# A trunk layer on one Trainium2 core: its loads bound to program order on the sync queue

## The chip, the cores and the metric

One NeuronCore of a Trainium2 chip runs the whole program. The metric is the device time of one execution in microseconds (us). The kernel before takes 1918.01 us in the median of 3 runs (1916.22 to 1918.19). The engines are named as in the profile: PE (TensorE), PEld (its weight loads), DVE (VectorE), ACT (ScalarE), POOL (GpSimd), and SP (SyncE), which here only issues DMAs.

## What is computed

One layer for 512 tokens of width 2048: sliding-window attention with grouped keys and a learned sink, then a gated feed-forward part with a causal convolution of width 3, each between two RMS norms and with a residual. The part that the change touches is the second:

```python
def conv_ffn(h, w_up, conv_w, w_down):
    S = h.shape[1]
    u = h @ w_up                                   # 512x2048 @ 2048x11264
    up = jnp.pad(u, ((0, 0), (CONV_WIDTH - 1, 0), (0, 0)))
    c = conv_w[0] * up[:, 0:S]
    for j in range(1, CONV_WIDTH):
        c = c + conv_w[j] * up[:, j:j + S]
    gate, val = jnp.split(c, 2, axis=-1)
    return (jax.nn.silu(gate) * val) @ w_down      # 512x5632 @ 5632x2048
```

All is float32. The kernel splits every matrix into a high part `wh` (what PE's fast 32-bit format holds) and a rest `wl`, and forms each product with three matmuls: high by high, high by low, low by high (`prod`, L88 to L92; the matmuls all carry L83).

## The kernel before

Attention and its output projection come first (until about 510 us). Then come two stages. **Up stage**: the 5632 gate and value columns are made in 44 groups of 128, f = 0 to 43. Groups 4 to 43 are made by `up_pair(f, g)`, with a scheme of Strassen's kind: seven products of half size in place of eight. A pair (the gate and the value columns of f) loads four blocks of 128x1024 weights (`block`, tile `bw`, six buffers, 512 KB each), makes seven forms of them with DVE adds into a tile `raw`, splits each form into `wh` (ACT, L64) and `wl` (DVE, L65) in a ring of five slots, and multiplies each by a prepared form of the activations: 7 x 8 x 3 = 168 matmuls with 256 columns. Results are copied from PSUM by ACT (`s1`, `s2`, `s3`, `s7` at L672, `uv` at L704). At its end `gate` (L572 to L579) convolves both halves (`c0`, `c1`: one ACT step at L567, two DVE steps at L568 and L569 each), applies the SiLU on ACT (L574), multiplies on DVE (L576) and stores the result from SP into the DRAM tensor `hd` (L578).

**Down stage**: seven products of the same scheme again. Their weight operands are rows of the down matrix (`in_wdn`) and sums of them. These sums were made during the earlier stages, for each of the 22 row pairs kp, and stored in the DRAM tensor `td`: four loads of 512 KB into tiles `ts` (a pool of four), four adds, four stores. `weight_sums` adds on DVE (L144); `queue_sums` lets the DMA add into its target (L151, L152). In the up stage every five groups start one set of each kind: `weight_sums` at i = f - 4 = 0, 5, ..., 35 ahead of the pair, `queue_sums` after pair i = 1, 6, ..., 36; kp 6 to 21 are made so. All of these loads, adds and stores are issued by POOL. After the last set the `ts` pool is closed, its room becomes the tile `hq10`, and `fetch` brings the first activations of the down stage there. In the down stage `weight_form` loads `raw` (four buffers) and `fetch` loads the rest of the activations (`hq`), one piece every second kp.

What sets the order: matmuls are bound to the order in which they are traced (`keep_in_program_order`, in `mm`). Every other instruction is placed by a scheduler, which may move it ahead of others on its engine as far as its data and buffers allow. Each engine then works through its own list in that fixed order and waits at an instruction whose inputs are not there. SP does so too: a DMA issue that waits holds up those behind it.

Of the kernel before, what the change touches and what calls it, by code (L numbers as in the profile page):

```python
# [14 lines left out]
ALU = mybir.AluOpType  # L15
# [26 lines left out]
def trunk(ctx, tc, xT, x, grow, table, onehot, masked, sinks, conv,  # L42
          wkv, wq, wo, wup, wdn, out):
    nc = tc.nc
# [12 lines left out]
    def bank(i):  # L57
        return ps.tile([P, 512], F32, name=f"b{i}", bufs=1)
# [4 lines left out]
    def split(hi, lo, src):  # L63
        nc.scalar.activation(hi, src, AF.Copy)  # L64
        nc.vector.tensor_tensor(lo, src, hi.bitcast(F32), ALU.subtract)  # L65

    def halves():
        p = ring["slots"][ring["next"] % len(ring["slots"])]
        ring["next"] += 1
        return p.tile([P, 1024], F32R, name="wh"), p.tile([P, 1024], F32R, name="wl")  # L70
# [64 lines left out]
    hd = dr.tile([2, 2, P, NP, HALF], F32, name="hd")  # L135
    td = dr.tile([NP, P, 4, 1024], F32, name="td")

    def weight_sums(kp, sums):
        t = [sums.tile([P, 1024], F32, name="ts") for _ in range(4)]
        for q in (0, 2, 1, 3):  # L140
            nc.gpsimd.dma_start(t[q], wdn[4 * kp + q])
        yield
        for q, o in ((2, 0), (0, 1), (1, 2), (3, 1)):
            nc.vector.tensor_tensor(t[q], t[q], t[o], ALU.add)  # L144
            nc.gpsimd.dma_start(td[kp, :, q, :], t[q])
            yield

    def queue_sums(kp, sums):
        t = [sums.tile([P, 1024], F32, name="ts") for _ in range(4)]
        for q, other in ((2, 0), (0, 1), (1, 2), (3, 1)):  # L150
            nc.gpsimd.dma_start(t[q], wdn[4 * kp + q])  # L151
            nc.gpsimd.dma_start(t[q], wdn[4 * kp + other] if q in (0, 2) else t[other], accum_op=ALU.add)  # L152
            nc.gpsimd.dma_start(td[kp, :, q, :], t[q])

    def step(g, n=1):
        for _ in range(n):
            next(g, None)

    with ExitStack() as att:
# [10 lines left out]
        with ExitStack() as ph:  # L170
# [26 lines left out]
            for kt in range(KT):  # L197
                if kt == 0:
                    for h in range(2):
                        r = first[:, KT:] if h == 0 else pa.tile([P, 512], F32, name="xs")  # L200
                        c = KT + h * S
                        nc.sync.dma_start(r if h else first, xT[:, c if h else 0:c + S])
                        if h == 0:
                            w = halves()
                            raw = wraw.tile([P, 1024], F32, name="raw")
# [4 lines left out]
                elif kt % 2 == 0:  # L210
                    r = pa.tile([P, 1024], F32, name="xr")
# [205 lines left out]
        for u in range(NKV * NT):  # L417
            t = Unit(u)
# [28 lines left out]
    with ExitStack() as op:  # L447
        sums = op.enter_context(pool("tso", 4))
# [5 lines left out]
        g1 = gp.tile([P, D], F32, name="g1")  # L454
# [42 lines left out]
        def oproj(d, o):  # L497
            for u in range(8):
                w = weights(wo, 8 * d + u)
                for b in range(NT):  # L500
                    for k in range(2):
                        kt = 2 * u + k
                        prod(o[b], station(b, kt), wide(w, k), kt == 0, kt == KT - 1)
                if u % 4 == 0:
                    g = weight_sums(2 * d - 2 + u // 4, sums)
                step(g, (1, 0, 2, 3)[u % 4])
            for b in range(NT):
                evac_m(b, d, o[b])
# [9 lines left out]
        for b, bk in enumerate((2, 5, 6, 7)):  # L518
            o = bank(bk)
            for kt in range(KT):  # L520
                prod(o, station(b, kt), wide(ws[kt // 2], kt % 2), kt == 0, kt == KT - 1)
                if b > 1:
                    turn_tok(b - 2, kt, (0, 1, 3, 4))
                if b < 2:
                    if kt == 0:
                        g = weight_sums(4 + b, sums)
                    if kt in (0, 9, 11, 13, 15):
                        step(g)
            evac_m(b, 3, o)
            xn[b] = finish_tok(b)  # L530

        wu = {(h, u): weights(wup, 2 * h + u) for h in range(4) for u in range(2)}
        o = [bank(k) for k in (0, 1, 2, 5)]
# [18 lines left out]

    def fetch(m, par, g0, g1):
        t, k0 = next((t, k) for t, k, k1 in hq[m, par] if k <= g0 < k1)
        nc.sync.dma_start(t[:, g0 - k0:g1 - k0, :], hd[m, par, :, g0:g1, :])

    with ExitStack() as us:
        fp = us.enter_context(pool("fp", 1))
# [93 lines left out]
        sums = tsu.enter_context(pool("tsu", 4, side="right"))  # L652

        def block(f, r, c):
            t = bw.tile([P, 1024], F32, name="bw")
            nc.sync.dma_start(t, wup[4 * f + 2 * c + r])
            return t

        def form(t):
# [15 lines left out]
        def up_pair(f, g):  # L675
            X, Y, Z = (bank(k) for k in ((0, 1, 6), (3, 4, 7))[f % 2])
            ug = un.tile([P, S], F32, name="ug", bufs=2)
            uv = un.tile([P, S], F32, name="uv", bufs=2)
            b11, b21 = block(f, 0, 0), block(f, 1, 0)
            t = wraw.tile([P, 1024], F32, name="raw")  # L680
            nc.vector.tensor_tensor(t, b11, b21, ALU.add)
            times(X, 2, form(t), True)
            s1 = shot(X, "s1")
            step(g)
            b12 = block(f, 0, 1)
            times(Z, 7, form(b12), True)
            s7 = shot(Z, "s7")
            nc.vector.tensor_tensor(t, t, b12, ALU.add)
            times(X, 5, form(t), False)
            s2 = shot(X, "s2")  # L690
            step(g)
            nc.vector.tensor_tensor(b11, b11, b12, ALU.add)
            times(Z, 6, form(b11), False)
            b22 = block(f, 1, 1)
            nc.vector.tensor_tensor(t, t, b22, ALU.add)
            times(X, 3, form(t), False)
            s3 = shot(X, "s3")
            step(g)
            nc.vector.tensor_tensor(ug[:, :HALF], Z[:, :HALF], s2, ALU.subtract)
            times(Y, 1, form(b21), True)  # L700
            nc.vector.tensor_tensor(uv[:, :HALF], s3, s7, ALU.subtract)
            times(X, 4, form(b22), False)
            nc.vector.tensor_tensor(ug[:, HALF:], s1, Y[:, :HALF], ALU.subtract)
            nc.scalar.activation(uv[:, HALF:], X[:, :HALF], AF.Copy, scale=-1.0)  # L704
            gate(f, (ug, uv))

        kp = 6
        for f in range(4, NF):
            i = f - 4
            if i % 5 == 0 and kp < NP:  # L710
                work = weight_sums(kp, sums)
                step(work)
                kp += 1
            up_pair(f, work if i % 5 == 1 else iter(()))
            if i % 5 == 1:
                step(work)
            if i % 5 == 1 and kp < NP:
                queue_sums(kp, sums)
                kp += 1
            if kp == NP and tsu:  # L720
                tsu.close()
                tsu = None
                early = ctx.enter_context(pool("early", 1, side="right"))
                hq[1, 0] = [(early.tile([P, 16, HALF], F32, name="hq10"), 0, 16)]
                for g0, g1 in batches[:4]:
                    fetch(1, 0, g0, g1)
# [38 lines left out]
    def weight_form(src, kp):  # L765
        raw = raws[kp % 2].tile([P, 1024], F32, name="raw")
        table, q = src
        nc.sync.dma_start(raw, td[kp, :, q, :] if table else wdn[4 * kp + q])
        hi, lo = halves()
        split(hi, lo, raw)  # L770
        return hi, lo
# [5 lines left out]
    def product(o, form, src, fresh, tail=0):  # L777
        kept = []
        for g0, g1 in batches:
            af = act_form(*form, g0, g1)  # L780
            for kp in range(g0, g1):
                wf = weight_form(src, kp)
                if coming and kp % 2 == 0:
                    fetch(*coming.pop(0))
                if kp >= NP - tail:
                    kept.append((kp, af, g0, wf))
                    continue
                for t in range(2):
                    for e in range(2):
                        multiply(o, kp, af, g0, wf, t, e, fresh)  # L790
        return kept
# [13 lines left out]
    sums = {}  # L805
# [121 lines left out]
```

## Time and profile before

| | us |
|---|---|
| median of 3 runs | 1918.01 |
| the profiled execution, whole | 1915.05 |
| the profiled execution, first to last instruction (span) | 1913.3 |
| PE busy in the span | 1862.9 |
| DVE busy | 1455.1 |
| ACT busy | 980.9 |
| POOL busy | 125.9 |

All durations are taken from the profiled execution; its own time is 1.8 us more than its span and 3 us less than the median. The up pairs run from about 625 to 1458 us, the down stage from there to the end. PE's granted clock is a share of 2.4 GHz: 1.00, or 0.50 at the lower level. Where an engine is idle, the profile names what released it.

### The profile page before, as it was taken

How to read it: one execution, taken by the hardware profiler on the slowest of the kernel's cores; microseconds unless marked ns; L12 is line 12 of the kernel's file. 1: busy time of each engine (PE TensorE's matmuls, PEld its weight loads, DVE VectorE, ACT ScalarE, POOL GpSimd, SP SyncE). 2: the span in 40 equal slices, each digit the busy share in tenths (PEclk: the TensorE clock that was granted, in tenths of full speed). 3: DMA queues.
4: the chain of work that ended last, by engine and by line, in shares of the span. 5: the costliest groups of instructions: out<-in, count | busy, mean ns of one | idle time of the engine just before them, and what ended most of it. 6: DMA issues, size and time to landing. Idle time of an engine off the chain costs nothing.

```text
span 1913.3 us, 30053 instructions
## 1 busy us (share of the span) xinstructions
PE 1862.9 (97%) x11822; PEld 1689.4 (88%) x11822; DVE 1455.1 (76%) x2047; ACT 980.9 (51%) x1566; POOL 125.9 (7%) x216
## 2 busy tenths in 40 slices
PE   9999999999999999999999999999996899999998
PEld 7888888888899999998999999999996788888886
DVE  5468888745788979987898988888885466666875
ACT  7357777622344535444454555555553455545553
POOL 0000000012100222222222000000000000000000
PEclk9999999999999999999999999999998999999999
DMA  9533234499643889999999443333335766676773
GB/s 312 149 97 102 93 113 158 144 344 337 242 165 127 273 280 321 304 312 301 329 306 303 166 127 111 126 124 112 127 99 214 261 196 202 189 234 192 236 249 119
DMA packets 120845, 392.02 MB, mean 205 GB/s; under 512 B 13216, under 2 KB 26752, under 8 KB 118784
## 3 DMA queue, kind: packets, MB, share of 16 engines
q1 hardware_dynamic: 86720, 271.84, 42.2%
q0 software_dynamic: 29952, 109.07, 17.8%
q10 hardware_dynamic: 4032, 9.21, 1.6%
q8 instruction: 92, 1.51, 0.3%
q14 instruction: 49, 0.40, 0.1%
HBM read 309.29 MB, written 72.39 MB: 199 GB/s over the span
## 4 chain that ended last, share of the span: by engine, by line
PE 68%; DMA 16%; issue 9%; DVE 6%; ACT 1%; POOL 1%; DVEq 0%; SPq 0%; ACTq 0%; POOLq 0%
PE b L83 66%; DMA ts<-in_wdn 4%; DMA bw<-in_wup 3%; DMA ts<-ts 2%; DVE wl L65 2%; DMA raw<-in_wo 2%; PE b L86 1%; DMA td<-ts 1%; ACT wh L64 1%; DVE ts L144 1%; DMA hq<-hd 1%; DMA raw<-td 0%; DMA raw<-in_wup 0%; DVE xt L482 0%; DVE c L569 0%
## 5 line engine op out<-in xcount | busy, mean ns | idle before, releaser
L64 ACT ACTIVATE wh<-raw 128x1024 fp32r<-128x1024 f32 (+1 forms) x371 | 388.2, 1055 | 489.9 <-PE b L83 267.4
L65 DVE TENSOR_TENSOR wl<-raw,wh 128x1024 fp32r<-128x1024 f32 (+1 forms) x371 | 449.3, 1219 | 231.7 <-ACT wh L64 231.0
L83 PE MATMUL b<-ah,wh 128*128 128x256 f32 (+1 forms) x1824 | 561.9, 308 | 0.9 <-ACT s L672 0.5
L83 PE MATMUL b<-ah,wl 128*128 128x256 f32 (+1 forms) x1824 | 555.8, 305 | 5.9 <-DVE wl L65 5.9
L83 PE MATMUL b<-al,wh 128*128 128x256 f32 (+1 forms) x1824 | 554.4, 304 | 0.4 <-DVE al L65 0.4
L83 PEld LDWEIGHTS b<-ah,wl 128*128 128x128 f32 x1824 | 348.8, 191 | 22.3 <-DVE wl L65 7.7
L83 PEld LDWEIGHTS b<-ah,wh 128*128 128x128 f32 x1824 | 349.3, 192 | 13.2 <-ACT wh L64 2.0
L83 PEld LDWEIGHTS b<-al,wh 128*128 128x128 f32 x1824 | 349.4, 192 | 11.0 <-DVE al L65 0.6
L83 PE MATMUL b<-wh 128*128 128x512 f32 x616 | 241.7, 392 | 19.9 <-ACT wh L64 19.4
L83 PE MATMUL b<-wl,wh 128*128 128x512 f32 x616 | 241.9, 393 | 1.2 <-DVE wl L65 1.2
L83 PE MATMUL b<-wh,wl 128*128 128x512 f32 x616 | 241.4, 392 | 0.0
L64 ACT ACTIVATE wh<-bw 128x1024 fp32r<-128x1024 f32 x160 | 167.6, 1055 | 120.4 <-PE b L83 120.3
L65 DVE TENSOR_TENSOR wl<-bw,wh 128x1024 fp32r<-128x1024 f32 x160 | 194.3, 1219 | 7.6 <-ACT wh L64 7.0
L83 PEld LDWEIGHTS b<-wh 128*128 128x128 f32 x616 | 116.8, 190 | 45.6 <-ACT wh L64 20.3
L83 PEld LDWEIGHTS b<-wl,wh 128*128 128x128 f32 x616 | 116.7, 189 | 26.3 <-DVE wl L65 2.0
L83 PEld LDWEIGHTS b<-wh,wl 128*128 128x128 f32 x616 | 116.8, 190 | 24.2
L83 PE MATMUL b<-wh,ah 128*128 128x512 f32 x320 | 126.5, 395 | 0.0
L83 PE MATMUL b<-wh,al 128*128 128x512 f32 x320 | 124.8, 390 | 0.0
L83 PE MATMUL b<-wl,ah 128*128 128x512 f32 x320 | 124.6, 389 | 0.0
L144 DVE TENSOR_TENSOR ts<-ts 128x1024 f32<-128x1024 f32 x56 | 68.4, 1221 | 40.2 <-DMA ts<-in_wdn 31.8
L672 ACT ACTIVATE s<-b 128x256 f32<-128x256 f32 x160 | 59.3, 371 | 73.9 <-PE b L83 73.9
L83 PE MATMUL b<-f6h,wh 128*128 128x256 f32 x320 | 92.3, 288 | 5.0 <-ACT s L672 5.0
(165 smaller groups left out, 3099.4 us busy)
## 6 DMA issues: line engine op xcount, KB each, us to landing
bw<-in_wup SPq DMA_DIRECT2D x160, 512.0 KB, 4.8
ts<-in_wdn POOLq DMA_DIRECT2D x104, 512.0 KB, 8.3
td<-ts POOLq DMA_DIRECT2D x88, 512.0 KB, 5.5
raw<-td SPq DMA_DIRECT2D x88, 512.0 KB, 4.7
raw<-in_wdn SPq DMA_DIRECT2D x66, 512.0 KB, 4.2
raw<-in_wq SPq DMA_DIRECT2D x32, 512.0 KB, 3.6
raw<-in_wo SPq DMA_DIRECT2D x32, 512.0 KB, 4.8
hd<-c SPq DMA_DIRECT2D x44, 256.0 KB, 4.5
```

What stands on the lines that cost most here:

```text
L64: nc.scalar.activation(hi, src, AF.Copy)
L65: nc.vector.tensor_tensor(lo, src, hi.bitcast(F32), ALU.subtract)
L83: tc.keep_in_program_order(nc.tensor.matmul(o, l, r, start=start, stop=stop, skip_group_check=more))
L86: tc.keep_in_program_order(nc.tensor.transpose(o, src, ident))
L144: nc.vector.tensor_tensor(t[q], t[q], t[o], ALU.add)
L672: nc.scalar.activation(t, o[:, :HALF], AF.Copy)
```

## The change

A helper `in_turn` issues a DMA on SP and binds it behind the instruction that was traced just before it on SP. It is used for the `bw` loads, the down stage's `raw` loads, the activation loads of `fetch`, and the `ts` loads of the up stage, which leave POOL's queue for SP's. `queue_sums` issues its four loads first and its adds and stores after them in another order. The stores `hd` are not bound, nor are the weight sums of the stage before (kp 0 to 5). Line numbers behind the helper rise by 3 to 16.

```diff
+    def in_turn(o, i):
+        tc.keep_in_program_order(nc.sync.dma_start(o, i))
+
-    def weight_sums(kp, sums):
+    def weight_sums(kp, sums, paced=False):
         t = [sums.tile([P, 1024], F32, name="ts") for _ in range(4)]
         for q in (0, 2, 1, 3):
-            nc.gpsimd.dma_start(t[q], wdn[4 * kp + q])
+            (in_turn if paced else nc.gpsimd.dma_start)(t[q], wdn[4 * kp + q])
...
     def queue_sums(kp, sums):
         t = [sums.tile([P, 1024], F32, name="ts") for _ in range(4)]
-        for q, other in ((2, 0), (0, 1), (1, 2), (3, 1)):
-            nc.gpsimd.dma_start(t[q], wdn[4 * kp + q])
-            nc.gpsimd.dma_start(t[q], wdn[4 * kp + other] if q in (0, 2) else t[other], accum_op=ALU.add)
+        for q in (2, 0, 1, 3):
+            in_turn(t[q], wdn[4 * kp + q])
+
+        def add(q, o):
+            nc.gpsimd.dma_start(t[q], o, accum_op=ALU.add)
+
+        def store(q):
             nc.gpsimd.dma_start(td[kp, :, q, :], t[q])
+
+        add(2, wdn[4 * kp])
+        add(0, wdn[4 * kp + 1])
+        store(2)
+        add(1, t[2])
+        store(0)
+        add(3, t[1])
+        store(1)
+        store(3)
...
     def fetch(m, par, g0, g1):
-        nc.sync.dma_start(t[:, g0 - k0:g1 - k0, :], hd[m, par, :, g0:g1, :])
+        in_turn(t[:, g0 - k0:g1 - k0, :], hd[m, par, :, g0:g1, :])
...
         def block(f, r, c):
-            nc.sync.dma_start(t, wup[4 * f + 2 * c + r])
+            in_turn(t, wup[4 * f + 2 * c + r])
...
-                work = weight_sums(kp, sums)
+                work = weight_sums(kp, sums, True)
...
     def weight_form(src, kp):
-        nc.sync.dma_start(raw, td[kp, :, q, :] if table else wdn[4 * kp + q])
+        in_turn(raw, td[kp, :, q, :] if table else wdn[4 * kp + q])
```

What stands where, at three places. First SP's list around pairs 7 and 8. Pair 7 loads bw_6655, 6657, 6691 and 6783 and its gated product is c1_6881; pair 8 loads bw_6892, 6894, 6928 and 7020 (c1_7118); pair 9 loads bw_7137, 7139, 7173 and 7265; pair 10 begins with bw_7374 and 7376. Before:

```order
L656 DMA bw_6894<-in_wup 128x1024
L578 DMA hd_88<-c1_6389 128x2x256
L656 DMA bw_6928<-in_wup 128x1024
L656 DMA bw_7020<-in_wup 128x1024
L656 DMA bw_7137<-in_wup 128x1024
L656 DMA bw_7139<-in_wup 128x1024
L578 DMA hd_88<-c1_6644 128x2x256
L656 DMA bw_7173<-in_wup 128x1024
L656 DMA bw_7265<-in_wup 128x1024
L656 DMA bw_7374<-in_wup 128x1024
L656 DMA bw_7376<-in_wup 128x1024
L578 DMA hd_88<-c1_6881 128x2x256
```

After, at the same pairs:

```order
L139 DMA bw_6655<-in_wup 128x1024
L139 DMA bw_6657<-in_wup 128x1024
L139 DMA bw_6691<-in_wup 128x1024
L139 DMA bw_6783<-in_wup 128x1024
L594 DMA hd_88<-c1_6881 128x2x256
L139 DMA bw_6892<-in_wup 128x1024
L139 DMA bw_6894<-in_wup 128x1024
L139 DMA bw_6928<-in_wup 128x1024
L139 DMA bw_7020<-in_wup 128x1024
L594 DMA hd_88<-c1_7118 128x2x256
```

The store of a pair's product stood behind the first loads of three pairs later, and now stands between the pair's own loads and the next pair's.

Second, DVE's list at the end of pair 7 (ug_6653, uv_6654 are its results, c0_6876 and c1_6881 its gate) and the beginning of pair 8 (its forms are built in raw_6896). Before:

```order
L65 TENSOR_TENSOR wl_6899<-raw_6896,wh_6898 128x1024
L144 TENSOR_TENSOR ts_7127<-ts_7127,ts_7125 128x1024
L699 TENSOR_TENSOR ug_6653<-b7_6652,s2_6752 128x256
L65 TENSOR_TENSOR wl_6931<-bw_6928,wh_6930 128x1024
L701 TENSOR_TENSOR uv_6654<-s3_6814,s7_6721 128x256
L688 TENSOR_TENSOR raw_6896<-raw_6896,bw_6928 128x1024
L703 TENSOR_TENSOR ug_6653<-s1_6689,b4_6651 128x256
L681 TENSOR_TENSOR raw_7141<-bw_7137,bw_7139 128x1024
L65 TENSOR_TENSOR wl_6962<-raw_6896,wh_6961 128x1024
L65 TENSOR_TENSOR wl_6993<-bw_6892,wh_6992 128x1024
L568 SCALAR_TENSOR_TENSOR c1_6881<-uv_6654,cw_83,c1_6881 128x511
```

After:

```order
L584 SCALAR_TENSOR_TENSOR c0_6876<-ug_6653,cw_83,c0_6876 128x511
L585 SCALAR_TENSOR_TENSOR c0_6876<-ug_6653,cw_83,c0_6876 128x510
L584 SCALAR_TENSOR_TENSOR c1_6881<-uv_6654,cw_83,c1_6881 128x511
L585 SCALAR_TENSOR_TENSOR c1_6881<-uv_6654,cw_83,c1_6881 128x510
L592 TENSOR_TENSOR c1_6881<-c0_6876,c1_6881 128x512
L697 TENSOR_TENSOR raw_6896<-bw_6892,bw_6894 128x1024
L708 TENSOR_TENSOR bw_6892<-bw_6892,bw_6928 128x1024
L65 TENSOR_TENSOR wl_6899<-raw_6896,wh_6898 128x1024
```

Splits and sums of pair 8 stood among the last steps of pair 7; now the first of them stands behind pair 7's product, and ACT's list follows in the same way.

Third, SP's list where the last weight sums give way to `hq10`, at the entry into pair 41 (bw_14946). After:

```order
L139 DMA ts_14918<-in_wdn 128x1024
L139 DMA ts_14916<-in_wdn 128x1024
L139 DMA ts_14917<-in_wdn 128x1024
L139 DMA ts_14919<-in_wdn 128x1024
L139 DMA hq10_14936<-hd_88 128x1024 x4
L139 DMA bw_14946<-in_wup 128x1024
L139 DMA bw_14948<-in_wup 128x1024
```

Before, three of these hq10 loads stood among the loads of pairs 25 and 26 and the fourth some 40 rows later, since POOL had the sums done by then; the ts loads were not in SP's list.

## Rows read from the trace of the kernel before

**Rows 1.** Windows: length, busy us (instructions) of PE, PEld, DVE, ACT, POOL; clock; DMA.

```profile
690.00:1080.00 390.00, 371.75 (x3024) 368.61 (x3023) 341.11 (x377) 189.71 (x274) 82.99 (x136) 0.98 0.93 300
1080.00:1456.00 376.00, 375.65 (x3131) 375.45 (x3129) 318.32 (x351) 198.81 (x280) 0.00 (x0) 1.00 0.36 115
```

**Rows 2.** Waits of PE from 604 to 1456: us in total, times, longest.

```profile
PE b L83 <- ACT s L672: 9.9, 8, 3.3
PE b L83 <- DVE wl L65: 8.3, 6, 2.4
```

**Rows 3.** Waits of PE from 1456 to 1503, the change of stage.

```profile
PE b L83 <- ACT wh L64: 19.4, 2, 15.4
```

**Rows 4.** Timeline of SP in the quiet part: start us, us, instruction.

```profile
1162.64 0.38 SPq L578 DMA_DIRECT2D hd<-c  x1
...
1182.80 0.38 SPq L578 DMA_DIRECT2D hd<-c  x1
```

**Rows 5.** Waits of SP from 604 to 1456, at the stores.

```profile
SPq L578 <- DVE c L576: 48.0, 36, 3.7
```

**Rows 6.** Timeline of PE after pair 43.

```profile
1458.16 0.28 PE L83 MATMUL b<-f4h,wl 128*128 128x256 f32 x1
...
1477.35 0.79 PE L83 MATMUL b<-wh 128*128 128x512 f32 x1 [15.41 <-ACT wh L64]
```

**Rows 7.** Timelines of ACT, DVE and SP at the gate of pair 43.

```profile
1458.51 0.36 ACT L704 ACTIVATE uv<-b 128x256 f32<-128x256 f32 x1
1458.90 0.72 ACT L567 ACTIVATE c<-uv,cw 128x512 f32<-128x512 f32 x1
1460.79 0.63 ACT L574 ACTIVATE c<-c 128x512 f32<-128x512 f32 x1 [1.17 <-DVE c L569]
...
1460.67 0.74 DVE L568 SCALAR_TENSOR_TENSOR c<-uv,cw,c 128x511 f32<-128x511 f32 x1
1461.45 0.75 DVE L569 SCALAR_TENSOR_TENSOR c<-uv,cw,c 128x510 f32<-128x510 f32 x1
1462.31 0.69 DVE L576 TENSOR_TENSOR c<-c,c 128x512 f32<-128x512 f32 x1
...
1463.17 0.38 SPq L578 DMA_DIRECT2D hd<-c  x1
1463.59 2.60 SPq L555 DMA_DIRECT2D hq<-hd  x4
```

**Rows 8.** Tile bw from 604.4 to 608.3, a burst of loads: issues, and landing.

```profile
L656 SPq DMA_DIRECT2D bw<-in_wup x6: 327/456/919, 604.5 to 607.8; - x6
...
DMA to landing us min/median/max: 3.9/7.0/8.4
```

**Rows 9.** Tile bw from 1150 to 1260: ns min/median/max, first and last start.

```profile
L65 DVE TENSOR_TENSOR wl<-bw,wh x22: 1216/1220/1226, 1149.4 to 1256.2; 128x1024 fp32r<-128x1024 f32 x22
...
L692 DVE TENSOR_TENSOR bw<-bw x6: 1220/1224/1225, 1154.2 to 1255.1; 128x1024 f32<-128x1024 f32 x6
...
DMA to landing us min/median/max: 3.4/3.6/4.1
```

**Rows 10.** DMA issues from 640 to 1080: count, size, median us to landing.

```profile
bw<-in_wup SPq DMA_DIRECT2D x82, 512.0 KB, 7.0
...
td<-ts POOLq DMA_DIRECT2D x63, 512.0 KB, 6.3
ts<-ts POOLq DMA_DIRECT2D x16, 512.0 KB, 8.5
```

**Rows 11.** Windows at the lower clock and after it, columns as in rows 1.

```profile
697.00:703.80 6.80, 6.23 (x29) 6.23 (x30) 6.80 (x8) 3.17 (x6) 1.62 (x4) 0.50 0.59 198
703.80:711.00 7.20, 7.20 (x62) 7.20 (x62) 5.49 (x7) 0.53 (x2) 1.95 (x3) 1.00 0.97 284
...
908.60:915.40 6.80, 5.58 (x26) 5.58 (x27) 6.80 (x8) 0.48 (x2) 1.61 (x3) 0.50 0.79 280
...
1477.30:1482.00 4.70, 4.18 (x9) 3.00 (x10) 4.67 (x4) 2.95 (x3) 0.00 (x0) 0.50 1.02 413
```

## The prediction, on record before the change was run

> **What bounds the kernel now.** I read the windows by stage first. In the up stage TensorE (PE) is nearly always busy: 371.75 of 390 us while weight sums are also being made, 375.65 of 376 us after them [rows 1]. So only its waits can be won back there. The list of PE's waits gives them: 9.9 us for ScalarE (ACT) copies out of PSUM and 8.3 us for VectorE (DVE) splits [rows 2]. The third view is the change from the up to the down stage, where PE waits 19.4 us for weight halves, 15.4 of them at once [rows 3]. All of the rest is matmuls. One up pair (168 matmuls) lasts 20.16 us when nothing waits: that is the distance of two stores of gated activations [rows 4]. Between those stores PE never stops, because the loads of a pair run ahead of the pair before: bw has six buffers and a pair takes four.
>
> **What the change does to the queue.** Each bound load is put behind whatever was traced just before it on SP. At a pair's first load that is the store hd of the pair before, whose product is the last thing the pair makes. The order on SP shows it: before, the loads of pairs 8 and 9 and two of pair 10 stand ahead of the store of pair 7; now the store of pair 7 stands ahead of every load of pair 8. SP goes through its list in order and does wait at this store (36 waits in the up stage, for the DVE product) [rows 5]; those waits hurt nobody while loads stood ahead. The order on DVE and ACT follows: the sum of pair 8's first two blocks now stands behind pair 7's product. So at all 40 entries into an up pair (f = 4 to 43) nothing of the next pair is ready when PE ends its last matmul, and PE drains. I read this from the order, and price it from the trace.
>
> **The price of a plain entry.** The trace of before holds one such drain, at the end of pair 43: last matmul 1458.16 + 0.28 = 1458.44; 3.5 us later (1477.35 - 15.41 = 1461.94) the one block that was ready is used up, and PE stands until 1477.35 [rows 6]. Its steps, counted from the last matmul's end [rows 7]: the ACT copy uv starts at 0.07; the convolution's ACT step starts 0.39 later, and the SiLU (0.63) now stands between them; it lasts 0.72: 1.81. Two DVE convolution steps and the product go from 1460.67 to 1463.00, 2.33: 4.14. SP issues the store 0.17 later: 4.31, and its next DMA 0.42 after that: 4.73.
>
> Then loads. There is one burst of six bw loads on a quiet DMA, with one hd store among them [rows 8]: the first lands 3.9 us after its issue, the last at 607.8 + 8.4 = 616.2, that is 7.8 us after the first for five loads and half a load, 1.42 us each. The first form needs blocks one and two, but DVE's second instruction adds block three into block one and the split of the first form stands behind that. So the third load counts: 4.73 + 3.9 + 2 x 1.42 = 11.47. An add (1.22) and a split (1.22) follow [rows 9]: 13.9 us of idle PE.
>
> Then the clock. PE restarts at 1477.35 at a granted clock of 0.50 (1.2 GHz) and has 2.4 GHz again at 1482.0 [rows 6, 11]. At the lower level a 256-column matmul comes every 6.23/29 = 0.215 us, at the upper 7.2/62 = 0.117 [rows 11]; 4.7 us there lose 4.7 x (1 - 0.117/0.215) = 2.1. A plain entry costs 13.9 + 2.1 = 16.0 us. Three in five are plain: 24 x 16.0 = 384.
>
> The Trainium skill, TensorE: Matmul & The Clock Gate, section HAM oscillation, describes a kernel whose every tile restarts at the lower clock after a wait for data. By that rule all 40 entries pay the 2.1; if only this one place did, the sum would be 84 lower. The trace bears the rule out at this place and at 697 and 908.6.
>
> **Entries with weight sums in front.** Eight groups of five pairs make two sets of sums. Their four ts loads were on POOL's queue; they now stand on SP between the store and the next pair's loads, once per set: 16 entries. Four loads more before the third bw load: 4 x 1.42 = 5.7. POOL's queue moves the sums' stores and adds at the same time. While both queues were full, a bw load took 7.0 us [rows 10] against 3.6 in quiet [rows 9], so the share of that lies between 0 and 3.4; I take the middle, 1.7, since POOL has no loads left. 16.0 + 5.7 + 1.7 = 23.4, for 15 of them 351.
>
> The Trainium skill, DMA: Bandwidth & Descriptors, section Queues, rings and completion order, says that an engine goes round the queues that have work, a packet from each. By that the loads would get half the engines for as long as POOL has work, the upper end: 3.4 in place of 1.7, 26 us more over the 15. Rows 10 agree in kind.
>
> The sixteenth is the entry into pair 41: the loads hq10 stand there, in a tile over the room of the ts pool, so SP holds until the last sums are stored. First ts load 4.73 + 3.9 = 8.6; three adds that follow one another, 8.5 each [rows 10]: 34.1; a store, 6.3: 40.4; then four hq10 loads and three bw loads, 3.9 + 6 x 1.42 = 12.4: 52.8; add and split 2.4, clock 2.1: 57. Before, POOL was done by 1080 [rows 1], and nobody waited for this.
>
> **What is won.** The contention that delayed bw goes, with PE's 18.2 us [rows 2] and two spells of 6.8 us at the lower clock, 3.0 each [rows 11]: 24. At the change of stage the down weights no longer stand behind twelve hq loads: of 19.4 + 2.1 us I expect some 13 to stay, because block kp 0 is split only after the last gate and kp 1 is loaded after the last store: 8 won. In the down stage the loads keep their order but for neighbours that change places, and PE is the bound there: nothing. Instructions on PE, their number and order are the same.
>
> **Sum.** 384 + 351 + 57 = 792 lost, 24 + 8 = 32 won: 760 more. The profiled execution took 1915.05 us, 3 under the median of 1918.01: 1915 + 760 + 3 = **2678 us**.
>
> Lower bound of an entry: landing in 3.4 [rows 9], two loads enough for a start, 4.73 + 3.4 + 1.42 + 1.22 + 1.22 = 12.0, and no clock loss: 24 x 12.0 + 15 x 17.7 + 40 = 594, about 2480 in all. Upper bound: the store takes its half load's 0.7 first, a whole 6.8 us spell at the lower clock costs 3.0, sums 3.4: 17.6 and 26.7, the last 75: 898, about 2785.
>
> **The rivals.**
> - *The loads are paced and nobody drains.* If the first loads of a pair could go out before the store of the pair before is due, the change would only keep sums from crowding bw, and win its 24 + 8 us: about 1886. For it: SP's waits for the product summed to only 48 us [rows 5]. Against it: the order, in all 40 places, and DVE's order with it. It is decided by whether SP's first load of a pair is issued before or after the last matmul of the pair before. 4 in 100. No change at all: 1.
> - *The clock never recovers within a pair.* PE would work some 20 us and rest 14, and the lower level could hold through all 168 matmuls: 168 x (0.215 - 0.117) = 16.5, less the 2.1 counted, 14.4 x 40 = 576: about 3250. Against it: recovery 4.7 us after 15.4 of idling [rows 6, 11]. 6 in 100.
> - *The drain is real but shorter*, since first matmuls or the gate's steps overlap with something that I don't see: between 2000 and 2480: 7 in 100, mostly near the upper end.
>
> **How the numbers follow.** My forecast with its bounds has 82 in 100. The range is 2520 to 2810: the bounds with most of both ends, a little above the upper one, for the 16 entries with sums, whose price is a middle. About 0.2% is what a measurement of this kernel tells from no change. Faster by more: 0.04; within: 0.01; slower: 0.95.
>
> **What would show it.** Per pair, SP should issue hd and then four bw loads within 2 us, some 4.3 us after the last matmul; hd stores should lie 36 us apart, 43 with sums; PE's list of waits should be led by about 40 x 14 us or more in the up stage (wh and wl of the first form); the granted clock should fall in each drain; one pause of 55 us should stand before pair 41; POOL should issue 64 fewer loads; the down stage should last the same 410 us. Wrong would be: bw loads issued during the pair before, or PE without gaps in the up stage.

## The result, and the profile after

The changed kernel takes **2664.53 us** (median of 4 runs, 2660.88 to 2667.32), 1.389 times the kernel before (95% interval 1.387 to 1.392): 39% slower. 2678 was predicted. The profiled execution took 2660.88 us, its span is 2659.1 us. All line numbers from here on are those of the changed kernel, unless a kernel is said to be made from the one before.

From the page: PE's busy time, share and instructions; PE and its granted clock in 40 slices of the span; the chain that ended last, by engine.

```profile
PE 1964.8 (74%) x11822; PEld 1772.9 (67%) x11822; DVE 1486.4 (56%) x2047; ACT 982.1 (37%) x1566; POOL 91.5 (3%) x152
...
PE   9999999997466466566565665665665368999998
...
PEclk9999999998688678778777777777777688999999
...
PE 71%; DMA 13%; DVE 8%; ACT 3%; SPq 3%; issue 2%; POOL 0%; DVEq 0%; ACTq 0%; POOLq 0%
```

PE has the same 11822 matmuls, and is busy 1964.8 us against 1862.9. Idle it is 2659.1 - 1964.8 = 694.3 us, against 50.4. Both rows of slices have a hole where the up pairs lie, and nowhere else. Two windows of the up stage, with the columns of [rows 1]:

```profile
690.00:1080.00 390.00, 225.60 (x1658) 219.95 (x1657) 185.83 (x197) 102.47 (x148) 15.81 (x24) 0.77 0.34 115
1080.00:1456.00 376.00, 222.17 (x1634) 216.90 (x1632) 178.40 (x190) 101.83 (x145) 15.89 (x24) 0.78 0.34 113
```

PE issues 1658 matmuls where it issued 3024, and DMA is used about a third (0.34): nothing is saturated, everything waits in turn. PE's waits from 604 to 2220 us (in total, times, longest) say on what, and SP's on its store:

```profile
PE b L83 <- ACT wh L64: 634.3, 40, 42.7
PE b L83 <- DVE wl L65: 39.2, 40, 3.1
PE b L83 <- ACT s L688: 1.1, 6, 0.2
...
SPq L594 <- DVE c L592: 1410.1, 40, 42.3
```

Forty times PE waits for the first `wh` of a pair: once for each of the 40 entries. Of the 9.9 us of waits for ACT copies in [rows 2], 1.1 are left. SP's wait at the store, 48.0 us in [rows 5], is now 1410 us; 40 waits, one per pair.

**One plain entry, followed through the engines.** It is the pair that begins at 1387 us; PE, ACT, DVE and SP in turn:

```profile
1374.45 0.28 PE L83 MATMUL b<-f4h,wl 128*128 128x256 f32 x1
1387.04 0.58 PE L83 MATMUL b<-ah,wh 128*128 128x256 f32 x1 [12.31 <-ACT wh L64]
...
1388.38 0.58 PE L83 MATMUL b<-ah,wl 128*128 128x256 f32 x1 [0.54 <-DVE wl L65]
...
1375.56 0.71 ACT L583 ACTIVATE c<-uv,cw 128x512 f32<-128x512 f32 x1
1385.93 1.06 ACT L64 ACTIVATE wh<-raw 128x1024 fp32r<-128x1024 f32 x1 [9.66 <-DVE raw L697]
...
1377.88 0.69 DVE L592 TENSOR_TENSOR c<-c,c 128x512 f32<-128x512 f32 x1
1384.67 1.23 DVE L697 TENSOR_TENSOR raw<-bw 128x1024 f32<-128x1024 f32 x1 [6.10 <-DMA bw<-in_wup]
1385.97 1.23 DVE L708 TENSOR_TENSOR bw<-bw 128x1024 f32<-128x1024 f32 x1
1387.11 1.22 DVE L65 TENSOR_TENSOR wl<-raw,wh 128x1024 fp32r<-128x1024 f32 x1
...
1378.60 0.38 SPq L594 DMA_DIRECT2D hd<-c  x1
1379.03 1.90 SPq L139 DMA_DIRECT2D bw<-in_wup  x4
1414.67 0.38 SPq L594 DMA_DIRECT2D hd<-c  x1
1415.15 1.85 SPq L139 DMA_DIRECT2D ts<-in_wdn  x4
1417.09 2.49 SPq L139 DMA_DIRECT2D bw<-in_wup  x4
```

The last matmul ends at 1374.73. The gate's last step ends at 1378.57, the store goes out at 1378.60 (3.87 us after the matmul), the four loads from 1379.03 on. They land 1.25 to 1.29 us apart; DVE adds the first two at 1384.67, ACT splits at 1385.93, and PE runs again at 1387.04. The next pair's store is 36 us later. Before that next entry four `ts` loads stand in front of the bw loads, and hold them back another 1.94 us at issue and more in the DMA engines.

The clock around this restart, columns as in [rows 11]:

```profile
1387.04:1393.51 6.47, 5.92 (x26) 5.63 (x27) 5.35 (x6) 2.93 (x4) 0.00 (x0) 0.50 0.00 0
1393.51:1410.60 17.09, 17.09 (x144) 17.08 (x143) 7.87 (x10) 5.07 (x8) 0.00 (x0) 1.00 0.00 1
```

After the drain PE works 6.47 us at the lower level (1.2 GHz) and issues 26 matmuls there; in the next 17.09 us at 2.4 GHz it issues 144. The granted clock falls 40 times between 604 and 2220 us, once per entry.

### The profile page after: what moved, and what is told of

Same layout as the page of the kernel before. It is cut to its first block, busy times and chain, and to the rows that moved or that the text cites. A ratio compares the mean times of both kernels' runs of the same rounds, so it can differ in the third digit from the quotient of the medians.

```text
span 2659.1 us, 29985 instructions
## 1 busy us (share of the span) xinstructions
PE 1964.8 (74%) x11822; PEld 1772.9 (67%) x11822; DVE 1486.4 (56%) x2047; ACT 982.1 (37%) x1566; POOL 91.5 (3%) x152
## 4 chain that ended last, share of the span: by engine, by line
PE 71%; DMA 13%; DVE 8%; ACT 3%; SPq 3%; issue 2%; POOL 0%; DVEq 0%; ACTq 0%; POOLq 0%
PE b L83 70%; DMA bw<-in_wup 12%; SPq L139 2%; DVE bw L708 2%; DVE wl L65 2%; PE b L86 1%; DVE c L585 1%; DVE c L584 1%; DVE c L592 1%; ACT c L590 1%; ACT c L583 1%; DVE raw L697 1%; ACT wh L64 1%; SPq L594 1%; DMA raw<-td 0%
## 5 line engine op out<-in xcount | busy, mean ns | idle before, releaser
L83 PE MATMUL b<-ah,wh 128*128 128x256 f32 (+1 forms) x1824 | 607.7, 333 | 634.3 <-ACT wh L64 634.3
L83 PEld LDWEIGHTS b<-ah,wh 128*128 128x128 f32 x1824 | 391.0, 214 | 654.1 <-ACT wh L64 643.5
L83 PE MATMUL b<-ah,wl 128*128 128x256 f32 (+1 forms) x1824 | 598.2, 328 | 39.2 <-DVE wl L65 39.2
L65 DVE TENSOR_TENSOR wl<-raw,wh 128x1024 fp32r<-128x1024 f32 (+1 forms) x371 | 449.8, 1220 | 272.2 <-ACT wh L64 271.9
L83 PE MATMUL b<-al,wh 128*128 128x256 f32 (+1 forms) x1824 | 592.2, 325 | 0.4 <-DVE al L65 0.4
L83 PEld LDWEIGHTS b<-ah,wl 128*128 128x128 f32 x1824 | 386.2, 212 | 66.2 <-DVE wl L65 51.5
L83 PEld LDWEIGHTS b<-al,wh 128*128 128x128 f32 x1824 | 390.6, 214 | 10.9 <-DVE al L65 0.6
L697 DVE TENSOR_TENSOR raw<-bw 128x1024 f32<-128x1024 f32 x40 | 49.0, 1225 | 296.3 <-DMA bw<-in_wup 296.0
L65 DVE TENSOR_TENSOR wl<-bw,wh 128x1024 fp32r<-128x1024 f32 x160 | 191.6, 1218 | 0.0
```

The source lines that it names most:

```text
L83: tc.keep_in_program_order(nc.tensor.matmul(o, l, r, start=start, stop=stop, skip_group_check=more))
```

## Experiments

The theory of the prediction is that a pair's bound loads stand on SP behind the store of the pair before. The rivals after the result: the `ts` loads on SP are the cause; the down stage's bound loads are; a load bound in program order is slow in itself. All ratios are against runs of the kernel before on the same chip, with 95% intervals.

### Taking the store out of the way, in two ways, and binding bw alone

**bw unbound in the changed kernel.**

```diff
-            in_turn(t, wup[4 * f + 2 * c + r])
+            nc.sync.dma_start(t, wup[4 * f + 2 * c + r])
```

> The changed kernel with only the bw loads of the up pairs unbound again; the ts, hq and raw loads stay bound on SP. Its order has the first loads of a pair ahead of the store hd of the pair before once more, with the ts loads behind the stores. Theory (a pair's loads held behind the store of the pair before): the 40 drains go, PE waits under 40 us in the up stage, hd stores about 20.2 us apart; 1880 to 1930 us, some tens of us above that if the sixteen sets of ts loads still hold SP back. Rival (the ts loads, now in SP's queue, are what fills it and delays bw): the sets are still there, so the time stays above 2200 us. Rival (binding the down stage's loads is the cause): nothing changes, about 2660 us.

Measured: 1873.77 us, 0.979 (0.978 to 0.981). One line takes away the whole loss and leaves a kernel that is 2.1% **faster** than the one before. PE on its page, and all that PE waits for from 604 to 1430 us:

```profile
PE 1854.7 (99%) x11822; PEld 1683.7 (90%) x11822; DVE 1454.5 (78%) x2047; ACT 984.3 (53%) x1566; POOL 91.5 (5%) x152
...
PE b L83 <- ACT s L688: 1.7, 3, 0.8
```

The sums' loads are still on SP and bound, and cost nothing; so the first rival, the `ts` loads, falls as the main cause, and the second, the down stage's binding, with it.

**bw bound in the kernel before, and nothing else.**

```diff
-            nc.sync.dma_start(t, wup[4 * f + 2 * c + r])
+            in_turn(t, wup[4 * f + 2 * c + r])
```

> The kernel before with only the bw loads bound; all weight sums stay on POOL's queue, and the down stage's loads stay free. Its order has the store hd of a pair ahead of the next pair's loads, as in the changed kernel. Theory: 40 plain drains, of 13.0 us idle and some 2.5 to 2.9 us of lower clock each as in the changed kernel (16 x 40 = 640), no ts loads in front of 15 of them and no 43 us pause for hq10, and 24 us of the old waits gone: 2490 to 2570 us; the entries in the first half, where POOL moves sums, a few us dearer than those in the second. Rival (ts loads on SP): 1900 to 1930 us, since none is on SP. Rival (down stage): 1918 us.

Measured: 2575.56 us, 1.345 (1.343 to 1.347), 6 us above the range. The same one line, alone, makes nearly the whole loss. PE drains at 38 entries; the very first waits 6.8 us and one not at all. The 30 after POOL's sums are done idle 12.0 to 13.1 us each. The 8 before that idle 17 to 22 us, not a few us more but some 8, which is where the range was missed. Landing of four bw loads at such an early entry (issued at 787 us), and at a late one (1307 us), min, median and max:

```profile
DMA to landing us min/median/max: 10.3/14.6/15.9
...
DMA to landing us min/median/max: 4.1/5.7/6.9
```

The early four share the DMA engines with the sums on POOL's queue. That agrees with the Trainium skill, DMA: Bandwidth & Descriptors, section Queues, rings and completion order, by which a DMA engine goes round the queues that have work.

**The store on POOL, every load bound.**

```diff
-            nc.sync.dma_start(hd[:, par, :, kp, :].rearrange("m p t -> p m t"),
+            nc.gpsimd.dma_start(hd[:, par, :, kp, :].rearrange("m p t -> p m t"),
```

> The changed kernel, all its loads bound as they are, but the stores hd issued by POOL in place of SP: the bound loads then stand behind loads alone. Theory: no load waits for a gate any more; the six bw buffers let them run a pair ahead, the drains go, PE waits under 40 us in the up stage; 1870 to 1930 us, and the entry into pair 41 loses its pause for the most part. Rival (a load bound in program order is slow in itself, or the ts loads take the time): drains of 12 us or more stay, at least at the 16 entries with sums: above 2100 us.

Measured: 1906.46 us, 0.996 (0.994 to 0.997). With the bindings all in place and the store out of SP's list the drains are gone, so a bound load is not slow in itself. One remains, of the same kind. PE's first wait in the up stage, and SP's waits that go with it:

```profile
642.03 0.58 PE L83 MATMUL b<-ah,wh 128*128 128x256 f32 x1 [18.34 <-ACT wh L64]
...
SPq L139 <- DVE wl L65: 640.3, 146, 8.9
SPq L139 <- DVE al L617: 36.4, 1, 36.4
```

At the first pair, bw stands behind the first `ts` load, whose tile reuses room that DVE still needed until 626 us (`al`, L617): a bound load is held by whatever holds the one ahead, here a buffer and not a store. The 640 us that SP waits for `wl` are harmless: there it waits for a free bw buffer, with loads already ahead of PE. This run's span is 30 us longer than that of the run with bw unbound; the pause at the first pair with the short waits right behind it (21.4 us in all) and one of 4.1 us behind the hq10 loads are most of that.

### The place of the ts loads

The four `ts` loads of each set moved behind the bw loads of a pair:

```diff
             b22 = block(f, 1, 1)
+            if behind:
+                behind()
...
+            behind = None
             if i % 5 == 0 and kp < NP:
                 work = weight_sums(kp, sums, True)
-                step(work)
+                behind = lambda: step(work)
                 kp += 1
-            up_pair(f, work if i % 5 == 1 else iter(()))
+            if i % 5 == 2 and kp < NP:
+                behind = lambda k=kp: queue_sums(k, sums)
+                kp += 1
+            up_pair(f, work if i % 5 == 1 else iter(()), behind)
             if i % 5 == 1:
                 step(work)
-            if i % 5 == 1 and kp < NP:
-                queue_sums(kp, sums)
-                kp += 1
```

> The changed kernel, every load bound, but each set's four ts loads written behind the four bw loads of a pair (pairs i = 0 and 2 of five) in place of ahead of them; SP's list then has hd, bw x4, ts x4. The drains stay. In the changed kernel a plain pair takes 36.0 us (12.4 idle at the entry, 23.6 of matmuls), one with weight_sums ahead 42.2, one with queue_sums ahead 46.5, and the entry into pair 41 idles 42.7. Theory (what those entries cost more is the place of four loads on SP ahead of the bw loads): they become plain, 8 x 6.2 + 7 x 10.5 = 123 us less, and the pause for hq10 shrinks by some 20 because the last sums have a whole pair to finish: 2664 - 143 = about 2520, 2495 to 2550 us. Rival (the sums' traffic itself slows the bw loads, wherever the loads stand): less than 40 us is won, above 2620 us.

Measured: 2512.56 us, 1.310 (1.306 to 1.313), 152 less than the changed kernel. PE's waits in its up stage:

```profile
PE b L83 <- ACT wh L64: 495.0, 40, 13.3
PE b L83 <- DVE wl L65: 21.8, 40, 0.6
```

All 40 entries are now plain: 495.0 / 40 = 12.4 us, the longest 13.3. The hq10 loads now stand before pair 42, and neither that entry nor the one into pair 41 idles more than the rest, so the pause went wholly, not by 20. The sums' transfers are the same in both kernels and 152 us are won, so it is not that they slow the bw loads wherever the loads stand. With their loads, though, the adds and stores moved too: none of the 32 adds and 64 stores runs beside a bw load here, where in the changed kernel most do. This run takes away both, the place in the queue and the traffic beside, and does not tell one from the other.

### How much lead the loads need

Three versions keep every load bound and the store on SP, but let the next pair's four loads go ahead of it.

**The whole gate written behind the next pair's loads.**

```diff
-        def up_pair(f, g):
+        def up_pair(f, g, after=None):
...
             b11, b21 = block(f, 0, 0), block(f, 1, 0)
+            b12 = block(f, 0, 1)
+            b22 = block(f, 1, 1)
+            if after:
+                gate(*after)
...
-            b12 = block(f, 0, 1)
...
-            b22 = block(f, 1, 1)
...
-            gate(f, (ug, uv))
+            return f, (ug, uv)
```

> The changed kernel with every load bound and the stores hd still on SP, but each pair's four bw loads written ahead of the gate of the pair before: the same bindings, in another program order. SP then has bw of pair f+1, hd of pair f, bw of f+2. Theory: what costs is only that the store stands between; with the loads ahead of it four to six blocks are there when PE ends a pair: no drain at plain entries, 1880 to 1950 us (a store still holds the loads of the pair after next, which have 20 us to land). Rival (bound loads or ts loads are the cause): 2400 us or more.

Measured: 2080.38 us, 1.087 (1.085 to 1.088): outside both ranges. The plain entries do not drain, but those with `ts` loads in front do, by 2 to 8 us, the very first by 17 and the one into pair 41 by 25. At those with `ts` loads in front the bw loads went out 5 to 12 us before they were needed, not the 20 of my expectation, and took 7 to 18 us to land.

**Only the store's issue written later, the gate left where it was.**

```diff
-            nc.sync.dma_start(hd[:, par, :, kp, :].rearrange("m p t -> p m t"),
+            return lambda: nc.sync.dma_start(hd[:, par, :, kp, :].rearrange("m p t -> p m t"),
...
             b22 = block(f, 1, 1)
+            if store:
+                store()
```

> The changed kernel, every load bound, the stores hd still on SP and the gate where it was; only the store's issue is written later, behind the four bw loads of the next pair. SP's list is then bw of f+1, hd of f, (ts), bw of f+2: the same list as where the whole gate was written behind the next pair's loads, which took 2080 us with each store issued 11.5 us into the next pair and 15 entries 4 to 8 us idle. Here the gated product is ready some 4 us into the next pair, so the loads behind it, and the four ts loads ahead of those at 15 entries, have about 16 us. Theory (what counts is how long before the pair's first matmul its loads come free on SP): no drain at any of the 40 entries but the first and the one for hq10; 1870 to 1905 us. Rival (a set of ts loads ahead of bound bw loads costs its 5 us or more at any lead): 15 entries stay idle and the time is above 2000 us.

Measured: 2080.75 us, 1.085 (1.082 to 1.088). Missed again, and for the same reason. A stretch of SP, and of DVE at one gate; then what PE waits for at the first `wh` of a pair in the whole up stage:

```profile
874.95 0.38 SPq L594 DMA_DIRECT2D hd<-c  x1
875.43 1.85 SPq L139 DMA_DIRECT2D ts<-in_wdn  x4
877.38 2.85 SPq L139 DMA_DIRECT2D bw<-in_wup  x4
...
869.51 0.74 DVE L585 SCALAR_TENSOR_TENSOR c<-ug,cw,c 128x510 f32<-128x510 f32 x1
870.17 1.22 DVE L65 TENSOR_TENSOR wl<-raw,wh 128x1024 fp32r<-128x1024 f32 x1
871.31 0.74 DVE L585 SCALAR_TENSOR_TENSOR c<-uv,cw,c 128x510 f32<-128x510 f32 x1
871.97 2.35 DVE L65 TENSOR_TENSOR wl<-bw,wh 128x1024 fp32r<-128x1024 f32 x2
874.24 0.68 DVE L592 TENSOR_TENSOR c<-c,c 128x512 f32<-128x512 f32 x1
...
PE b L83 <- ACT wh L64: 108.6, 16, 25.2
```

Once the next pair's blocks are there, its splits (L65) run between the gate's steps on DVE, so the product is done at 874.9, 12 us after that pair's start (863.0). Where the store's issue is written changes nothing as long as its data come that late. PE's next pair was due at 883.4, and with the `ts` loads ahead of them the bw loads went out only at 877.38: PE idled 7.49 us there.

**Both: the store later, and ts behind bw.** (The two diffs above together.)

> Both moves at once: every load bound, hd on SP and written behind the next pair's four bw loads, and each set's ts loads behind a pair's bw loads too, ahead of that store. With the store alone written later the gated product came 9 to 11 us into the next pair, not the 4 I had reckoned with, because the next pair's splits now stand ahead of the gate's steps on DVE; its time, 2081 us, was that of the kernel with the whole gate written later. There the 24 plain entries do not drain, the entries with ts loads in front idle 2 to 7.5 us and another 2 to 4 right after, and the first entry 16 and the one into pair 41 25. Theory (a pair's loads have a lead of 8 to 10 us, which four loads keep and eight do not): without ts loads in front those entries stop draining, about 105 us of idling and 40 of lower clock less: 1915 to 1955 us, what is left over the kernel with unbound bw loads being mostly the first entry and the pause before pair 41. Rival (any bound load behind a store costs at these entries): above 2030 us.

Measured: 1967.95 us, 1.023 (1.018 to 1.028): 113 less, 13 above the range. The idle time before `wh` falls from 108.6 to 28.6 us; 15.8 of it is the pause behind the hq10 loads, which stand before pair 42 here, and 6.8 the very first entry. Six entries keep 3 to 5.5 us, waits for `wl` included. The wait for `wh` in the up stage, then the landing of the four bw loads before an entry without such a wait (issued at 1327 us), and before one with it (1347 us):

```profile
PE b L83 <- ACT wh L64: 28.6, 8, 15.8
...
DMA to landing us min/median/max: 4.2/5.4/6.6
...
DMA to landing us min/median/max: 7.7/11.3/13.8
```

The second group shares the DMA with the adds and stores of `queue_sums`, whose loads came a pair earlier. So traffic does cost: at these six entries the bw loads go out 12 us before they are needed, and the four need 8 to 14 to land. It is most of what is left here, beside the two pauses; in the changed kernel it is a part of what the entries behind `queue_sums` cost.

### What the change gains beside the drains

**Only the sums changed in the kernel before** (their loads bound on SP, and the new order in `queue_sums`).

```diff
-            nc.gpsimd.dma_start(t[q], wdn[4 * kp + q])
+            (in_turn if paced else nc.gpsimd.dma_start)(t[q], wdn[4 * kp + q])
...
-        for q, other in ((2, 0), (0, 1), (1, 2), (3, 1)):
+        for q in (2, 0, 1, 3):
+            in_turn(t[q], wdn[4 * kp + q])
```

> The kernel before with only the weight sums changed: their loads bound on SP, and the new order of loads, adds and stores; bw, hq and raw loads stay free. Theory (the gain that shows once the drains are gone comes from the sums no longer crowding the bw loads): PE's waits in the up stage, 18.2 us, and the two spells at the lower clock go: 1885 to 1900 us. Rival (the gain lies in the down stage's bound loads): 1910 to 1920 us.

Measured: 1889.83 us, 0.986 (0.983 to 0.988), 27.0 less than before.

**Only the down stage's loads bound in the kernel before.**

```diff
-        nc.sync.dma_start(raw, td[kp, :, q, :] if table else wdn[4 * kp + q])
+        in_turn(raw, td[kp, :, q, :] if table else wdn[4 * kp + q])
...
-                    fetch(*coming.pop(0))
+                    fetch(*coming.pop(0), bound=True)
```

> The kernel before with only the down stage's loads bound (raw, and the hq pieces fetched beside them; the first hq10 loads stay free). Theory: the pause of 15.4 us at the change of stage shrinks to some 4, since the first down weights no longer stand behind twelve hq loads: 1900 to 1908 us. Rival (the change of stage was short in the changed kernel only because its drains left DMA and SP empty): 1914 to 1920 us. If binding the down stage had caused the slowdown it would be above 2000 us.

Measured: 1903.07 us, 0.992 (0.989 to 0.995), 13.8 less. PE's waits from 604 to 1480 us in these two, the sums first:

```profile
PE b L83 <- ACT wh L64: 19.5, 2, 15.9
PE b L83 <- ACT s L688: 2.4, 3, 1.1
PE b L83 <- DVE wl L65: 1.2, 2, 0.8
...
PE b L83 <- DVE wl L65: 9.9, 8, 3.1
PE b L83 <- ACT s L675: 9.1, 5, 3.3
PE b L83 <- ACT wh L64: 5.9, 2, 3.0
```

Each takes away its own waits and leaves the other's: with the sums on SP the waits of [rows 2] go and the pause of [rows 3] stays; with the down loads bound the pause shrinks from 15.4 to 3.0 and the others stay. 27.0 + 13.8 = 40.8 us, and the changed kernel with bw unbound gains 1914.7 - 1873.8 = 40.9. That the two agree to 0.1 us is luck, since the six runs with the down loads bound alone lie up to 11 us apart; that the gains add up is not.

## Why the prediction was right, step by step

**The mechanism** is the one named, and it is shown: unbinding bw undoes the loss, binding bw alone makes nearly all of it, and with the store off SP's list every binding may stay (1906 us). Order on SP decided it; the long view of [rows 5], 48 us of waits at the store, spoke the other way, because there loads stood ahead.

**The sum.** The changed kernel and the one with bw unbound differ by 2659.1 - 1874.8 = 784.3 us of span, 674.2 of it PE idle and 110.1 PE busy at the lower clock; 792 was forecast as lost. The won part is 1913.3 - 1874.8 = 38.5 of span; 32 was forecast. That the total came so near owes something to luck: the entries with sums cost 10 us more than forecast and the one into pair 41 11 us less. By terms, each measured as an entry's mean idle time (for a plain one 12.43 us, and 0.60 right behind its first matmuls) plus the time from there to the pair's end, less the 20.16 us of [rows 4]:

| term | predicted, us | measured, us |
|---|---|---|
| plain entry, idle | 13.9 | 12.43 + 0.60 = 13.0 |
| plain entry, clock | 2.1 | 23.57 - 0.60 - 20.16 = 2.8 |
| 24 plain entries | 384 | 380 |
| entry with sums, DVE adding (8) | 23.4 | 17.72 + 24.48 - 20.16 = 22.0 |
| entry with sums, DMA adding (7) | 23.4 | 21.64 + 24.97 - 20.16 = 26.4 |
| these 15 | 351 | 361 |
| entry into pair 41 | 57 | 42.7 + 23.2 - 20.16 = 45.7 |
| won in the up stage | 24 | 27.0 (alone) |
| won at the change of stage | 8 | 13.8 (alone) |

**Plain entry.** Two of its steps were off and partly cancelled. The steps of the gate were right to 0.4 us (3.87 to the store, 4.31 forecast). I let PE wait for the third load, an add and a DVE split; the first matmul needs only the second load, an add and ACT's split (1.06). The third load landed at 1385.87, while DVE was at that add; what delays the third matmul, by 0.54 us, is the second add, which stands on DVE ahead of its split. The loads lay 1.26 us apart, not 1.42, but the first took 4.3 us to land, not 3.9. The clock term was too small: from PE's restart to the rise of the granted clock it took 6.2 us in the mean of the 40 restarts (4.3 to 8.7), where [rows 11] had 4.7 at one. That every restart pays it is the rule of the Trainium skill, TensorE: Matmul & The Clock Gate, section HAM oscillation; this trace agrees, with 40 falls at 40 entries and 110 us / 40 = 2.75 us each. (From [rows 11] a matmul at the upper level takes 0.116 us, not the 0.117 that I used; that moves the term by 0.02 us.)

**Entries with sums.** One price stood for two kinds. The four loads ahead cost 6.2 us more than a plain entry where DVE adds later (5.7 + 1.7 forecast), and 10.6 where the DMA adds: POOL issues the first adds as soon as the first `ts` tile is there, and they run beside the bw loads. At 1495 us the second bw load took 10.5 us to land, at 1417 us, in the other kind, 8.1. The share of POOL's traffic, 1.7 as a middle between 0 and 3.4, is the term that was mis-sized: with the four loads at their 5.7 it is 0.5 in one kind and 4.9 in the other, above the most that I allowed.

**The pause before pair 41** was there, for the reason given: SP holds the hq10 loads until the sums are stored. Its rows on SP, and the wait between the second and the third of them:

```profile
2083.41 0.38 SPq L594 DMA_DIRECT2D hd<-c  x1
2083.84 1.89 SPq L139 DMA_DIRECT2D ts<-in_wdn  x4
2109.58 1.75 SPq L139 DMA_DIRECT2D hq<-hd  x4
2111.38 2.12 SPq L139 DMA_DIRECT2D bw<-in_wup  x4
...
SPq L139 <- DMA td<-ts: 23.4, 1, 23.4
```

From the first `ts` load to the hq10 loads it takes 25.7 us; 3.9 + 3 x 8.5 + 6.3 = 35.7 was forecast. The adds of `ts` tiles by DMA now take a median of 5.0 us in place of 8.5 [rows 10]; I priced them from a crowd that is gone. POOL's queue being free of loads is not all of it: with that the median is still 7.4 where bw is unbound and 7.9 where only the sums were changed. What does the rest is not shown.

**The change of stage.** PE's two pauses after pair 43, in place of 15.41 us in [rows 6] and another 4.04 after it, are 2.98 and 3.98 us:

```profile
2220.78 0.50 PE L83 MATMUL b<-wh 128*128 128x512 f32 x1 [2.98 <-ACT wh L64]
...
2230.90 0.80 PE L83 MATMUL b<-wh 128*128 128x512 f32 x1 [3.98 <-ACT wh L64]
```

I had kept 13 us there, for a load of kp 1 behind the last store. The binding of the down stage wins most of the pause on its own (13.8 us in the run with it alone). From the last up pair's end to the end of the program it is 441.3 us against 454.9.

The rivals: loads do not go out ahead of the store; the clock recovers in every pair; the drain is as long as forecast. POOL issues 152 instructions against 216, the 64 fewer that were named.

**My expectations during the study** failed where I guessed a lead instead of reading it: twice I took the store's time in a new order from the old order's gate.

## What to carry to other kernels

Before binding a load into program order, look at what was traced just ahead of it on its queue: if that is a store of the previous step's last result, or a load into room that is still in use, the load's lead is gone and the engine that it feeds drains (here at every pair behind the store, and at one behind the load). Bind loads behind loads, and keep such stores off their queue: with the store on POOL's queue every load could stay bound, at 0.4% under the kernel before, and with the pair's own loads unbound and the others bound the time was 2.1% under it. A wait of SP is harmful only if the loads behind it have less lead than they take to land: read the lead from the trace of the order in question, for moving one issue also moves the steps that feed it.

## What the runs showed of the hardware

Two accumulating DMAs from POOL's queue slowed the loads beside them on SP's nearly as much as four further loads ahead of them on SP: 512 KB took 4.3 to 6.6 us in a quiet entry, 7.6 to 11.5 behind four loads (the later ones beside stores from POOL), and 7.2 to 14.9 with two adds beside as well; the second load of each four took 5.0, 8.1 and 10.5. After the 40 drains of 12 to 43 us PE worked 4.3 to 8.7 us at the lower level before the granted clock rose, 6.47 at the entry shown; the 4.7 after the 15.4 us pause of the kernel before [rows 11] lies within that. What sets the length is left open.
